# Scaling k, q and v weights inside their high/low split, column by column of the norm weight

## Chip, cores and metric

One core of one Trainium2 chip. The time is that of one execution on the device, in microseconds. All data is float32.

## The reference

A two-layer decoder trunk on 1024 tokens of width 1024. Layer 0 is gated linear attention and a gated MLP with a causal convolution of width 3. Then one shared K and V is projected from the stream, and layer 1 is differential attention on it (8 heads, two softmax maps each) and a second MLP. Each projection reads a normed stream, and the norms here have a weight per channel:

```
def rmsnorm(x, w):
    y = x * rsqrt(mean(x * x, axis=-1) + EPS)
    return y * w
kv = rmsnorm(h, kv_norm_w) @ w_kv            # -> k (rotary), v
q  = rope(rmsnorm(h, attn_norm_w[1]) @ w_q)
```

The channel weight w multiplies rows of w_kv and w_q, so it can be taken into them. The kernel does so for k, q and v, because k and v have one norm weight and q another while all three read the same stream.

## The kernel before

Activations are kept transposed, channels on the 128 partitions. A float32 product is made of three products of rounded parts (`fp32r`): each operand is split into a high part, made by a ScalarE copy into `fp32r`, and a low part, the rest, made by VectorE's `scalar_tensor_tensor` (helper `lo_of`, recorded at L114): low = x * scale - high. TensorE then accumulates high*high, low*high and high*low in PSUM (`proj_half`, L275 to L277; `v_block`, L1188 to L1190).

**Weights.** `plan` lists every weight tile in the order of use. `emit_load` issues its DMA into one of four `raw` buffers; `emit_split` makes (wh, wl) from it; `take` returns the oldest finished pair and calls `prefetch`, which splits and loads ahead (one ahead during the attention). A tile is 128x1024: for k and q it holds the eight channel blocks (k = 0 to 7) of 128 output columns, for v two channel blocks of 512 columns. The plan's entry (gi, k0, nk) names the norm weight, the first block and the number of blocks: (G_KV, 2j, 2) for eight tiles of v, (G_KV, 0, 8) and (G_ATTN1, 0, 8) for eight tiles each of k and q. `gains_sb[:, gi, d]` is a column of 128 norm weights. For these 24 tiles VectorE first multiplies the raw tile in place by the broadcast columns (L194, recorded at L111 as `raw<-raw,gains_sb`), then ScalarE copies the whole tile to wh (L195) and VectorE writes wl.

**Order.** ScalarE, TensorE and the DMA queue (SP) run in the order in which the program is written (`manual_schedule`). VectorE and GpSimd are put in order by a planner, which works with its own estimates of durations and with the program's order as priority, so that a VectorE instruction can be placed well ahead of its neighbours in the source.

**The attention stage.** After v (v_unit, 16 blocks) and k and q of heads 0 and 1, a loop over 64 steps (8 heads of 8 query blocks) does, in each step: the scores of block i two steps ahead into two PSUM buffers (`scores`, tile `sp`), the transposes of the weights (`turn`, tiles `tp`, `ah`, `al`), the combining of the two maps (`combine`, VectorE, tile `e`), and `weights`: VectorE's maximum of each map (`mx`) and ScalarE's exponential (`e`), after which the PSUM buffers are free for later scores. Into the steps are spread the projections of k and q of heads 2 to 7 in half units (`rope_unit`, tile `pf`), 8 units a head. The first unit of a projection calls `take`, which makes the split of the next tile. GpSimd does the rest of the rotary (`xw<-xw,sinr`, `y<-y,xw`, 128x1024) and the low parts of each head's q, k and v (`xl`).

Of the kernel before, what the change touches and what calls it, by code (L numbers as in the profile page):

```python
# [12 lines left out]
AF = mybir.ActivationFunctionType  # L13
ALU = mybir.AluOpType
AX = mybir.AxisListType

P = 128
# [30 lines left out]
def trunk(  # L48
# [26 lines left out]
    PE, ACT, DVE, POOL = nc.tensor, nc.scalar, nc.vector, nc.gpsimd  # L75
# [14 lines left out]
    def U(name, dt=F32):  # L90
        return up.tile([P, 1026], dt, tag="u", name=uid(name))[:, 0:1024]
# [18 lines left out]
    def tt(eng, o, a, b, op):  # L110
        eng.tensor_tensor(out=o, in0=a, in1=b, op=op)  # L111

    def stt(eng, o, a, s, b, op0, op1):
        eng.scalar_tensor_tensor(out=o, in0=a, scalar=s, in1=b, op0=op0, op1=op1)  # L114

    def lo_of(eng, lo, x, hi, scale=1.0):
        stt(eng, lo, x, scale, hi.bitcast(F32), ALU.mult, ALU.subtract)
# [5 lines left out]
    gains_sb = const.tile([P, 6, ND], F32, name="gains_sb")  # L123
# [6 lines left out]
    def gain(g, d):  # L130
        return gains_sb[:, g, d:d + 1]
# [30 lines left out]
    loaded, ready = deque(), deque()  # L162
# [3 lines left out]
    def emit_load():  # L166
        *srcs, g = plan[nxt[0]]
        nxt[0] += 1
        raws = []
        for src in srcs:  # L170
            raws.append(rawtile("raw"))
            nc.sync.dma_start(raws[-1], src)
        loaded.append((raws, g))

    def emit_split(eng=None):
        eng = eng or WENG
        if pair:
            emit_piece()
            return
        if not loaded:  # L180
            emit_load()
        raws, g = loaded.popleft()
        if g == "pair":
            pair.append(pieces(*raws) if len(raws) == 2 else pieces_by_form(raws[0:2], raws[2:4]))
            emit_piece()
            return
        raw, = raws
        hi = U("wh", F32R)
        lo = U("wl", F32R)
        if g is not None:  # L190
            gi, k0, nk = g
            rv = raw.rearrange("p (k n) -> p k n", k=nk)
            gb = gains_sb[:, gi, k0:k0 + nk].unsqueeze(2).broadcast_to([P, nk, 1024 // nk])
            tt(eng, rv, rv, gb, ALU.mult)  # L194
        ACT.activation(hi, raw, AF.Copy)  # L195
        if eng is POOL:
            tt(POOL, lo, raw, hi.bitcast(F32), ALU.subtract)
        else:
            lo_of(DVE, lo, raw, hi)
        ready.append((hi, lo))  # L200
# [21 lines left out]
    def pieces(ra, rg):  # L222


        a11, a12, s3, a22, s1, s2 = sums(ra, rg)
        yield halves(a11, "wp")
        yield halves(s2, "wp")
        tt(POOL, s2, a12, s2, ALU.subtract)
        yield halves(a12, "wp")
        yield halves(s3, "wp")  # L230
        yield halves(s1, "wp")
        yield halves(a22, "wp")
        pair.clear()
        yield halves(s2, "wp")

    def pieces_by_form(*raws):

        held[0] = True
        xs = [sums(*r) for r in raws]
        for q in (0, 1):  # L240
            for x in xs:
                yield halves(x[q], "wp")
        for a11, a12, s3, a22, s1, s2 in xs:
            tt(POOL, a12, a12, s2, ALU.subtract)
        for q in (1, 4, 5, 2, 3):
            held[0] = q == 1
            for x in xs:
                if q == 3 and x is xs[-1]:
                    pair.clear()
                yield halves(x[q], "wp")  # L250

    def emit_piece():
        ready.append(next(pair[0]))

    def prefetch(n, eng=None):
        while len(ready) < n and (pair or loaded or nxt[0] < len(plan)):
            emit_split(eng)
        while nxt[0] < len(plan) and (not loaded and not held[0] if plan[nxt[0]][-1] == "pair" else
                                      len(loaded) + len(ready) < max(n, LOADS)):
            emit_load()  # L260
# [237 lines left out]
    for d in range(ND):  # L498
        t = U("x")
# [309 lines left out]
    for hf in range(2):  # L809
        for d in range(ND):  # L810
# [7 lines left out]
            t = hx[d]  # L818
# [664 lines left out]
    for s in range(-2, steps + 5):  # L1483
        a, i = divmod(s + 2, NB)
# [5 lines left out]
        b, j = divmod(s - 1, NB)  # L1490
        if 0 <= s - 1 < steps and j % 2 == 1:
            heads[b].values(j // 2)
        b, j = divmod(s, NB)
        if 0 <= s < steps:
            heads[b].turn(j)
        if 0 <= s + 1 < steps:
            b, j = divmod(s + 1, NB)
# [19 lines left out]
        if 0 <= s - 2 < steps:  # L1517
            b, j = divmod(s - 2, NB)
# [4 lines left out]
        if 0 <= s - 3 < steps:  # L1523
            b, j = divmod(s - 3, NB)
            if j == NB - 1:
                heads[b].norm2()
        if 0 <= s - 4 < steps:
            b, j = divmod(s - 4, NB)
# [126 lines left out]
```

## Time and profile before

| | us |
|---|---|
| median of 3 runs | 2475.18 (2474.6 to 2475.31) |
| the profiled execution | 2473.61 |
| its span, first to last instruction | 2471.9 |
| TensorE busy | 2341.2 (95%) |
| VectorE busy | 1899.2 (77%) |
| ScalarE busy | 1039.0 (42%) |
| GpSimd busy | 837.4 (34%) |

PE is TensorE (PEld its weight loads), DVE VectorE, ACT ScalarE, POOL GpSimd. A row of a timeline gives the start and the length of an instruction, its engine, line and operation, out<-in, shapes, count, and in brackets the idle time of the engine before it with what ended it. Lengths include time in which a started instruction is held up. The attention stage lies between about 1240 and 1760 us.

### The profile page before, as it was taken

The page shows a single profiled execution, that of the slowest core. Times are in us where ns is not written, and L with a number is a line of the kernel's source. Part 1 is how long each engine was busy: PE and PEld are TensorE (multiplying, and loading weights), DVE is VectorE, ACT ScalarE, POOL GpSimd, SP SyncE. Part 2 cuts the span into 40 slices and gives each one's busy share as a digit, 9 for nine tenths or more (in the row PEclk, how much of TensorE's full clock was granted, in tenths as well). Part 3 has the DMA queues.
Part 4 walks back from the last instruction along what each step waited for, and adds up shares of the span by engine and source line. Part 5 has one row for each costly group of instructions (what it writes and reads, how often), then busy time and mean ns, then how long its engine had stood idle before and what let it go on. Part 6 is the DMA issues. An engine that isn't in the chain of part 4 may idle for free. (4 is left out here: it accounts for less than half of the span.)

```text
span 2471.9 us, 29625 instructions
## 1 busy us (share of the span) xinstructions
PE 2341.2 (95%) x10926; PEld 1888.5 (76%) x10926; DVE 1899.2 (77%) x2509; ACT 1039.0 (42%) x1856; POOL 837.4 (34%) x659
## 2 busy tenths in 40 slices
PE   8999999799999998999999999899789999998998
PEld 6878877577888886788877777787667888886786
DVE  7454454779999998957148888776779999999966
ACT  5433442433444344444124555544334433343453
POOL 3210101145554428400004444522036545436501
PEclk9999999899999999999999999999989999999999
DMA  4011224122333356324243333522113323256422
GB/s 178 1 52 69 70 93 149 42 68 95 111 110 99 111 200 230 117 71 165 81 138 106 107 111 95 182 75 94 67 34 120 119 82 111 92 192 222 144 88 98
DMA packets 101426, 271.22 MB, mean 110 GB/s; under 512 B 10273, under 2 KB 23201, under 8 KB 101281
## 3 DMA queue, kind: packets, MB, share of 16 engines
q1 hardware_dynamic: 101280, 269.34, 32.3%
q8 instruction: 85, 1.39, 0.2%
q14 instruction: 61, 0.49, 0.1%
HBM read 184.89 MB, written 76.02 MB: 106 GB/s over the span
## 5 line engine op out<-in xcount | busy, mean ns | idle before, releaser
L896 PE MATMUL pf<-xp,wp 128*128 128x512 f32 x1232 | 489.2, 397 | 37.4 <-ACT wp L205 33.2
L897 PE MATMUL pf<-xp,wp 128*128 128x512 f32 x1232 | 489.0, 397 | 7.1 <-DVE wp L114 7.1
L898 PE MATMUL pf<-xp,wp 128*128 128x512 f32 x1232 | 488.6, 397 | 0.0
L896 PEld LDWEIGHTS pf<-xp,wp 128*128 128x128 f32 x1232 | 233.1, 189 | 94.0 <-ACT wp L205 34.3
L897 PEld LDWEIGHTS pf<-xp,wp 128*128 128x128 f32 x1232 | 233.1, 189 | 64.3 <-DVE wp L114 9.1
L898 PEld LDWEIGHTS pf<-xp,wp 128*128 128x128 f32 x1232 | 233.0, 189 | 54.8
L1007 PE MATMUL out<-rp,lp 128*128 128x512 f32 (+1 forms) x632 | 251.1, 397 | 19.1 <-DVE rp L114 18.8
L1006 PE MATMUL out<-rp,lp 128*128 128x512 f32 (+1 forms) x632 | 250.1, 396 | 6.3 <-DVE lp L114 6.3
L114 DVE SCALAR_TENSOR_TENSOR c<-u,cv,c 128x1024 f32<-128x1024 f32 x176 | 244.7, 1392 | 7.6 <-ACT c L903 7.6
L1005 PE MATMUL out<-rp,lp 128*128 128x512 f32 (+1 forms) x632 | 249.9, 395 | 0.6 <-ACT rp L205 0.6
L111 DVE TENSOR_TENSOR u<-pf,u 128x512 f32<-128x512 f32 x300 | 200.4, 679 | 28.3 <-PE pf L898 20.1
L114 DVE SCALAR_TENSOR_TENSOR wp<-raw,wp 128x512 fp32r<-128x512 f32 x180 | 203.0, 1139 | 12.9 <-ACT wp L205 12.9
L275 PE MATMUL pf<-xh,wh 128*128 128x512 f32 x458 | 187.5, 409 | 10.7 <-ACT wh L195 9.7
L276 PE MATMUL pf<-xh,wl 128*128 128x512 f32 x458 | 181.9, 397 | 1.2 <-DVE wl L114 1.2
L277 PE MATMUL pf<-xl,wh 128*128 128x512 f32 x458 | 181.4, 396 | 0.0
L1007 PEld LDWEIGHTS out<-rp,lp 128*128 128x128 f32 x632 | 121.3, 192 | 51.6 <-DVE rp L114 24.6
L111 POOL TENSOR_TENSOR rs_y<-rs_m,nhalf 128x4 f32<-128x4 f32 (+2 forms) x26 | 31.9, 1226 | 370.9 <-DVE rs_m L291 301.7
L923 ACT ACTIVATE c<-c 128x1024 f32<-128x1024 f32 x44 | 46.7, 1061 | 255.7 <-DVE c L114 255.7
L114 DVE SCALAR_TENSOR_TENSOR wp<-wt,wp 128x512 fp32r<-128x512 f32 x128 | 153.6, 1204 | 0.0
L1006 PEld LDWEIGHTS out<-rp,lp 128*128 128x128 f32 x632 | 120.8, 191 | 36.8 <-DVE lp L114 9.8
L111 POOL TENSOR_TENSOR wt<-raw,wt 128x512 f32<-128x512 f32 x40 | 57.0, 1425 | 254.5 <-DVE wp L114 254.5
L1005 PEld LDWEIGHTS out<-rp,lp 128*128 128x128 f32 x632 | 121.3, 192 | 27.6 <-ACT rp L205 1.1
(252 smaller groups left out, 5170.5 us busy)
## 6 DMA issues: line engine op xcount, KB each, us to landing
raw<-in_w_in SPq DMA_DIRECT2D x88, 512.0 KB, 4.2
tr<-td SPq DMA_DIRECT2D x70, 512.0 KB, 4.1
td<-c SPq DMA_DIRECT2D x44, 512.0 KB, 2.8
wo<-in_w_out SPq DMA_DIRECT2D x44, 512.0 KB, 8.5
raw<-in_w_gla SPq DMA_DIRECT2D x24, 512.0 KB, 5.9
h<-hs SPq DMA_DIRECT2D x24, 512.0 KB, 6.5
td<-mt SPq DMA_DIRECT2D x22, 512.0 KB, 3.8
hs<-h SPq DMA_DIRECT2D x32, 256.0 KB, 2.0
```

The source lines that it names most:

```text
L111: eng.tensor_tensor(out=o, in0=a, in1=b, op=op)
L114: eng.scalar_tensor_tensor(out=o, in0=a, scalar=s, in1=b, op0=op0, op1=op1)
L275: PE.matmul(o, wh[:, k], xh[:, H(hf)], start=(k == 0), stop=False)
L276: PE.matmul(o, wl[:, k], xh[:, H(hf)], start=False, stop=False)
L277: PE.matmul(o, wh[:, k], xl[:, H(hf)], start=False, stop=(k == ND - 1))
L896: PE.matmul(o, wh, xh, start=(k == 0), stop=False)
L897: PE.matmul(o, wl, xh, start=False, stop=False)
L898: PE.matmul(o, wh, xl, start=False, stop=(k == ND // 2 - 1))
L923: ACT.activation(gt, gt, AF.Silu)
L1005: PE.matmul(o, wh, xh, start=(j == 0 or cut and j == NJ - LASTF), stop=False)
L1006: PE.matmul(o, wl, xh, start=False, stop=False)
L1007: PE.matmul(o, wh, xl, start=False, stop=(j == NJ - 1 or cut and j == NJ - LASTF - 1))
```

## The change

For a tile with a norm weight, the multiplication of the whole tile is gone. ScalarE makes the high part block by block, with the column of the norm weight as its scale, and VectorE the low part block by block, with the same column as its scalar: two blocks of 128x512 for v, eight of 128x128 for k and q, first all of ScalarE's, then all of VectorE's. The raw tile is no longer written. Other tiles are split as before.

```diff
         if g is not None:
             gi, k0, nk = g
-            rv = raw.rearrange("p (k n) -> p k n", k=nk)
-            gb = gains_sb[:, gi, k0:k0 + nk].unsqueeze(2).broadcast_to([P, nk, 1024 // nk])
-            tt(eng, rv, rv, gb, ALU.mult)
+            parts = [tuple(t.rearrange("p (k n) -> p k n", k=nk)[:, k] for t in (hi, lo, raw)) for k in range(nk)]
+            for k, (a, _, x) in enumerate(parts):
+                ACT.activation(a, x, AF.Copy, scale=gain(gi, k0 + k))
+            for k, (a, b, x) in enumerate(parts):
+                lo_of(DVE, b, x, a, gain(gi, k0 + k))
+            ready.append((hi, lo))
+            return
         ACT.activation(hi, raw, AF.Copy)
```

## Rows read from the trace of the kernel before

**Rows 1.** The page's part 1: busy us (share of the span) xinstructions of each engine.
```profile
PE 2341.2 (95%) x10926; PEld 1888.5 (76%) x10926; DVE 1899.2 (77%) x2509; ACT 1039.0 (42%) x1856; POOL 837.4 (34%) x659
```
**Rows 2.** Stretches: length, busy us of PE, PEld, DVE, ACT, POOL; clock, DMA share, GB/s.
```profile
1150.00:1240.00 90.00, 90.00 (x397) 73.00 (x396) 20.43 (x30) 18.79 (x25) 1.01 (x1) 1.00 0.28 96
...
1330.00:1460.00 130.00, 125.44 (x801) 101.83 (x798) 108.25 (x172) 68.60 (x159) 55.48 (x42) 1.00 0.32 98
```
**Rows 3.** The same view in steps of 10 us, about 1300.
```profile
1300.00:1310.00 10.00, 5.89 (x28) 4.53 (x27) 8.65 (x10) 1.94 (x5) 3.30 (x2) 0.81 0.42 133
1310.00:1320.00 10.00, 10.00 (x53) 8.09 (x52) 7.56 (x10) 6.17 (x12) 5.72 (x4) 0.85 0.43 131
```
**Rows 4.** Groups by line, 1130 to 1900: busy us, mean ns | idle before, releaser.
```profile
L111 DVE TENSOR_TENSOR raw<-raw,gains_sb 128x1024 f32<-128x1024 f32 x24 | 42.1, 1762 | 11.4 <-DMA raw<-in_w_v 7.7 <-DMA raw<-in_w_k 3.7
...
L195 ACT ACTIVATE wh<-raw 128x1024 fp32r<-128x1024 f32 x32 | 34.0, 1069 | 34.7 <-DVE raw L111 34.6
```
**Rows 5.** Timeline of ACT: four scaled copies of 128x256 in the first stage.
```profile
110.02 1.71 ACT L698 ACTIVATE wg<-wg,ro 128x256 f32<-128x256 f32 x4 [2.49 <-DVE ro L111]
```
**Rows 6.** Timeline of DVE: operations of 128x128 and their neighbour.
```profile
1294.32 0.35 DVE L114 SCALAR_TENSOR_TENSOR e<-e,rc 128x128 f32<-128x128 f32 x1
...
1297.75 0.28 DVE L114 SCALAR_TENSOR_TENSOR al<-tp,ah 128x128 fp32r<-128x128 f32 x1
1297.94 0.21 DVE L114 SCALAR_TENSOR_TENSOR rc<-s,nlam,rc 128x1 f32<-128x1 f32 x1
```
**Rows 7.** Timeline of DVE in the first FFN.
```profile
604.74 1.18 DVE L114 SCALAR_TENSOR_TENSOR wp<-raw,wp 128x512 fp32r<-128x512 f32 x1
605.85 1.78 DVE L114 SCALAR_TENSOR_TENSOR wp<-wt,wp 128x512 fp32r<-128x512 f32 x1
```
**Rows 8.** Timeline of POOL there.
```profile
605.34 1.74 POOL L111 TENSOR_TENSOR raw<-raw,raw 128x512 f32<-128x512 f32 x1
```
**Rows 9.** Timeline of DVE in one head of the attention.
```profile
1342.32 1.21 DVE L114 SCALAR_TENSOR_TENSOR wl<-raw,wh 128x1024 fp32r<-128x1024 f32 x1
...
1365.14 2.78 DVE L114 SCALAR_TENSOR_TENSOR wl<-raw,wh 128x1024 fp32r<-128x1024 f32 x1 [0.56 <-ACT wh L195]
1367.84 0.94 DVE L1329 TENSOR_REDUCE mx<-sp 128x1 f32<-128x768 f32 x1
...
1370.23 3.42 DVE L111 TENSOR_TENSOR raw<-raw,gains_sb 128x1024 f32<-128x1024 f32 x1
```
**Rows 10.** Timeline of POOL in that head.
```profile
1364.24 2.60 POOL L111 TENSOR_TENSOR xl<-st,xh 128x1024 fp32r<-128x1024 f32 x1 [4.12 <-ACT xh L314]
...
1367.08 3.04 POOL L111 TENSOR_TENSOR xw<-xw,sinr 128x1024 f32<-128x1024 f32 x1
1370.21 2.37 POOL L111 TENSOR_TENSOR y<-y,xw 128x1024 f32<-128x1024 f32 x1
```
**Rows 11.** Timeline of PE in that head: rows with idle time.
```profile
1371.32 0.50 PE L1312 MATMUL sp<-xh,xh 64*128 64x512 f32 x1 [0.31 <-ACT e L1330]
...
1375.62 0.51 PE L275 MATMUL pf<-xh,wh 128*128 128x512 f32 x1 [0.33 <-DVE osb L114]
...
1379.18 0.50 PE L1312 MATMUL sp<-xh,xh 64*128 64x512 f32 x1 [0.50 <-ACT e L1330]
1380.19 0.49 PE L1312 MATMUL sp<-xh,xh 64*128 64x512 f32 x1 [0.51 <-ACT e L1330]
```
**Rows 12.** Timeline of PE in the last head with a split: rows with idle time.
```profile
1576.76 0.49 PE L1312 MATMUL sp<-xh,xh 64*128 64x512 f32 x1 [0.30 <-ACT e L1330]
...
1590.34 0.38 PE L1312 MATMUL sp<-xh,xh 64*128 64x256 f32 x2 [1.50 <-ACT e L1330]
```
**Rows 13.** Timeline of DVE in the first attention steps.
```profile
1300.98 2.81 DVE L114 SCALAR_TENSOR_TENSOR e<-e,rc 128x384 f32<-128x384 f32 x1
```
**Rows 14.** Timeline of POOL there.
```profile
1298.28 2.65 POOL L111 TENSOR_TENSOR xw<-xw,sinr 128x1024 f32<-128x1024 f32 x1 [13.32 <-DVE rc L114]
```
**Rows 15.** Timeline of PE there.
```profile
1306.52 0.79 PE L1312 MATMUL sp<-xh,xh 64*128 64x512 f32 x1 [4.11 <-ACT e L1330]
```

## The prediction

> **What bounds the kernel now.** I read the page's busy times first: TensorE is busy 95% of the span and VectorE 77% [rows 1], so a change to VectorE and ScalarE work can pay or cost only where TensorE waits for them. The table of stretches says where that is. All of v's projection (1150 to 1240) runs with TensorE busy 90.00 of 90 us while VectorE has 20.4 and ScalarE 18.8 us of work; from 1330 to 1460, where k's and q's projections are spread over the attention steps, TensorE idles 4.56 us and VectorE is busy 108 of 130 [rows 2]. The table in 10 us steps shows one worse spot: in 1300 to 1310 TensorE is busy 5.89 us and its granted clock falls to 0.81, then 0.85 [rows 3], below the upper of its two levels. So the 24 changed tiles fall in two sorts: eight of v, whose cost is hidden, and sixteen of k and q, most of them beside the attention.
>
> **Part by part.**
>
> *Removed:* 24 VectorE multiplications of 128x1024, mean 1.76 us [rows 4], although a VectorE split of the same size, with two SBUF sources too, takes 1.21 when nothing holds it [rows 9]. That is 42 us of VectorE. What makes them long is GpSimd: the multiplication at 1370.23 lasts 3.42 us, and GpSimd's y runs from 1370.21 for 2.37 [rows 9, 10]. VectorE instructions with two SBUF sources and GpSimd's tensor ops wait for each other whole.
>
> *ScalarE:* one copy of 1.07 us [rows 4] becomes, for k and q, eight of 128x128 with a column as scale. Four such of 128x256 span 1.71 us, 0.495 the single one [rows 5], so (1.71 - 0.495) / 3 = 0.405 from start to start; 128 columns fewer are about 0.1 ((1.07 - 0.495) / 768 per column), so 0.3 each and 2.4 a tile: 1.4 more. ScalarE next waits for the maxima of the scores, which are later still (below), so I take nothing for it; without that cover it would be 1.4 a tile.
>
> *VectorE's split:* one of 1.2 us alone becomes eight of 128x128. A split of that size starts 0.19 before the next instruction; an operation of that size with a column scalar and two SBUF sources lasts 0.35 whole [rows 6]. Between them I take 0.25 (0.19 to 0.35), so 2.0 a tile (1.5 to 2.8). [...]
>
> *v's eight tiles:* two instructions for one on each engine, one multiplication less. TensorE has no idle time there [rows 2], and VectorE and ScalarE are three quarters idle: nothing, either way.
>
> *The sixteen of k and q, the wait that counts.* Next to each split is a queue of GpSimd work (xl, then the rotary xw and y). In each of five heads (k's tile, split starting at 1315, 1365, 1417, 1468 and 1519, all of 2.77 or 2.78 us) the order is that of rows 9: the split, held by xl until 1366.71 (1365.14 + 2.78 - 1.21), then the maximum of the next scores at 1367.84, for which the exponentials and with them TensorE's score products wait: TensorE stands 0.31 at 1371.32 [rows 11]. There is no slack, so what the split adds goes to TensorE. xw asks at 1367.08 and gets its turn after 0.67 us (3.04 - 2.37), when the split is done [rows 10]. With eight pieces it need not wait: only one or two are done by 1367.08. Which goes first at such an instant is shown in the FFN: GpSimd asks at 605.34 while VectorE's split runs until 605.92; VectorE's next split, started at 605.85 without a pause, lasts 1.78 instead of 0.68, while GpSimd's operation lasts 1.74 [rows 7, 8]. The one that waits gets the next gap, even in a row of VectorE instructions. So xw goes between the pieces: 2.37 us, and then six pieces, 1.5: the maximum starts at about 1367.25 + 2.37 + 1.5 = 1371.1, 3.3 late. Below: if nothing cuts in, 1366.71 + 2.0, 0.9 late, or zero and less if the planner, which orders VectorE anew, puts the maximum ahead. Above: y cuts in too, another 2.37, 5.6 late. I take one cut, 3.3. [...]
>
> *What comes back:* with the multiplication at 1370.23 gone, 3.4 us of VectorE are free just behind the late maximum, so the next maxima are on time again and the stalls of 0.33, 0.50 and 0.51 [rows 11] go: 1.34. One head shows that already: its tile belongs to the output projection and has no multiplication, and after 0.30 at 1576.76 TensorE's next wait is at 1590.34 [rows 12]. The three rows recur in three of the five heads: 4.0 us.
>
> *q's tiles* lie where TensorE has room (1330 to 1460 holds two k tiles, whose stalls of rows 11 sum to 2 x 1.65 of the 4.56 idle in rows 2, and 0.6 a head is left for all else): nothing, at most one GpSimd operation of 2.37 each.
>
> *The first attention steps:* at 1300.98 a combine of 384 columns lasts 2.81 us beside GpSimd; the exponentials come late and TensorE waits 4.11 at 1306.52 [rows 13 to 15]. It starts right behind GpSimd's xw (1298.28 + 2.65 = 1300.93) and is then held by the next one. Ahead of it VectorE has a multiplication and a split, 2.4 us; after, 2.0 of pieces, while GpSimd is idle until 1298.28. So it comes 0.4 earlier or more, against a GpSimd start that waits for a transfer and doesn't move; the rows don't say whether that is enough to be ahead of it. If it is, 4.11 go and the lower clock with them (5.89 x 0.19 + 10 x 0.15 = 2.6): -6.7. If not, 0. I take half, -3.4.
>
> *Clock:* a stall of 3.6 in each head may bring the clock down as the 4.11 did: 0 to 5 x 2.6 = 13. I take 0, as the nearest row has the longer stall.
>
> *Sum:* 5 x 3.3 - 4.0 - 3.4 = +9.1. The profiled execution took 2473.6 (span 2471.9 and 1.7 around it): 2482.7. The median of the runs is 1.6 above it: 2484.
>
> **Rivals.**
> *A, the row of pieces isn't cut* (the planner puts the maxima ahead of them, or VectorE keeps its turn): the late maximum costs 0 to 0.9, the multiplications' 1.3 a head come back, the start stall goes: -4.0 - 6.7 = -10.7, 2464.5; with 0.9 a head, 2469. For it: 42 us less on the engine that ends TensorE's waits, and the head of rows 12. Against it: the FFN's rows 7 and 8.
> *B, all nearly cancels:* the cut costs 0.9 to 2 a head and is paid by the stalls that go: 5 x 1.5 - 4.0 - 3.4 = 0, 2475. For it: TensorE's waits there are 2.2 a head in all. Against it: no row has the maximum with slack.
> *C, the forecast's mechanism in full:* two cuts in each head and the clock with them, 5 x 5.6 - 4.0 + 13 = +37, 2512. It decides where y's request comes within one piece of xw's end; before, it came 0.09 after it (1367.08 + 3.04 to 1370.21).
>
> **How the numbers follow.** Forecast with its upper side C 0.50 (C alone 0.12), A 0.28, B 0.22. Up to 0.2%, 5 us, can't be told from no change. A is faster, B the same, the forecast and C slower: 0.28, 0.22, 0.50. The likeliest one's own range is 2478 (the start stall gone whole, 0.5 a head less) to 2497 (a clock fall in each head). The range for 8 in 10 reaches down to A's 2465 and up to 2503, most of the way to C.
>
> **What would show it.** Right: eight pieces of wl in a row between 1365 and 1372 with one piece of 2.5 us or more and xw beside it, the 768-column maximum 2 to 4 us later in the head, stalls of 2 to 4 us at the 896-column scores and none at the next. Wrong: pieces of 0.3 us throughout, xw waiting for several of them, or the maximum between them; TensorE's idle time in the attention under that of before. If v's stretch shows TensorE idle, or ScalarE is what the maxima's readers wait for, my terms of nothing fail.

## The result, and the profile after

The changed kernel takes 2506.03 us (median of 4 runs, 2505.21 to 2508.99); the kernel before, run beside it on the same chip, takes 2474.89 (2473.95 to 2475.31). The ratio is 1.0128, with an interval of 1.0115 to 1.0141: slower by 31 us. The profiled execution after took 2505.44 (span 2503.7), the one of before 2473.6 (span 2471.9), so the two profiles carry the difference: 31.8 in the span.

Part 1 of the page after: busy us, share of the span, instructions of each engine.

```profile
PE 2352.2 (94%) x10926; PEld 1902.5 (76%) x10926; DVE 1905.4 (76%) x2605; ACT 1060.5 (42%) x1976; POOL 825.5 (33%) x659
```

Read against [rows 1], this line splits the loss. TensorE does the same 10,926 matmuls and is busy 11.0 us longer (2352.2 - 2341.2). Its idle time is 2503.7 - 2352.2 = 151.5, where it was 2471.9 - 2341.2 = 130.7: 20.8 more. 11.0 + 20.8 = 31.8, the whole difference. VectorE lost 24 multiplications and is busy 6.2 us longer; GpSimd, whose work did not change, is busy 11.9 us less, because it waits less: xw and y of the rotary take 2.46 and 2.38 us in the mean where they took 2.74 and 2.82.

The stretch from the first score product to the end of the last `pv` product (1285.3 to 1702.3 before, 1285.8 to 1734.2 after) holds 2477 matmuls in both traces. First before, then after (length, busy us of PE, PEld, DVE, ACT, POOL; clock, DMA share, GB/s):

```profile
1285.30:1702.30 417.00, 392.04 (x2477) 318.60 (x2478) 332.80 (x545) 214.28 (x483) 161.02 (x119) 0.98 0.35 112
1285.80:1734.20 448.40, 400.03 (x2477) 329.75 (x2478) 349.25 (x611) 227.53 (x560) 151.60 (x119) 0.94 0.33 104
```

So 31.4 of the 31.8 us lie in the attention. There TensorE is busy 8.0 us longer for the same matmuls, at a mean granted clock of 0.94 instead of 0.98, and idle 23.4 longer (448.40 - 400.03 against 417.00 - 392.04). Of the 11.0 us above, 3.0 lie ahead of v's projection, where no changed tile is used, with 2.4 us less idle time: the two executions differ there. Any split into busy and idle time is only as good as the matmuls' modelled ends; the sum is exact.

The groups by line, 1130 to 1800, that stand where those of [rows 4] stood (busy us, mean ns | idle before, releaser):

```profile
L114 DVE SCALAR_TENSOR_TENSOR wl<-raw,gains_sb,wh 128x128 fp32r<-128x128 f32 x128 | 84.7, 722 | 5.7 <-ACT wh L194 5.7
L194 ACT ACTIVATE wh<-raw,gains_sb 128x128 fp32r<-128x128 f32 x128 | 39.1, 402 | 5.5 <-DMA raw<-in_w_k 5.5
```

A piece of 128 columns takes 722 ns in the mean, more than half of what a whole split of 1024 takes when nothing holds it (1.21 us, [rows 9]).

The stretches (length, busy us of PE, PEld, DVE, ACT, POOL; clock, DMA share, GB/s):

```profile
1150.00:1240.00 90.00, 90.00 (x398) 73.29 (x397) 14.66 (x40) 22.48 (x43) 1.01 (x1) 1.00 0.27 93
1330.00:1460.00 130.00, 115.68 (x731) 95.36 (x730) 103.83 (x181) 70.31 (x180) 47.58 (x39) 0.95 0.30 90
```

v's projection is as it was [rows 2]. From 1330 to 1460 TensorE gets through 731 matmuls where it did 801, with 14.3 us idle instead of 4.6 and a clock of 0.95 instead of 1.00. The same view in steps of 10 us, beside [rows 3]:

```profile
1300.00:1310.00 10.00, 8.48 (x48) 6.72 (x49) 7.58 (x13) 4.82 (x14) 1.17 (x1) 1.00 0.54 162
1310.00:1320.00 10.00, 6.39 (x38) 4.65 (x36) 9.81 (x13) 4.82 (x13) 7.57 (x5) 0.87 0.35 120
1320.00:1330.00 10.00, 7.50 (x37) 6.59 (x38) 6.35 (x11) 3.44 (x8) 0.00 (x0) 0.61 0.31 88
1370.00:1380.00 10.00, 4.75 (x27) 4.12 (x27) 10.00 (x13) 2.51 (x7) 6.09 (x5) 0.78 0.13 52
1380.00:1390.00 10.00, 10.00 (x64) 8.06 (x64) 7.51 (x14) 5.45 (x12) 0.90 (x1) 0.88 0.37 107
1430.00:1440.00 10.00, 4.77 (x24) 3.77 (x22) 9.30 (x16) 2.47 (x5) 2.81 (x2) 0.68 0.13 52
```

Each line with VectorE at 9.3 to 10.0 is a tile of k. TensorE works half to two thirds of such a stretch, and its granted clock is 0.87, 0.78 and 0.68 there, and 0.61, 0.88 and 0.98 (1440 to 1450) in the line behind it; between 1370 and 1390, in steps of 1 us, it is 0.50 from 1376 to 1382, and 1.00 up to 1375 and from 1383 on. Before, it was 1.00 in all of these stretches but the first two, those of [rows 3], where in steps of 1 us it was 0.50 from 1307 to 1313.

What happens in one head is in the timelines. VectorE, where [rows 9] stood (start us, us, engine, line, operation, out<-in, count, and in brackets the idle time ahead):

```profile
1292.82 1.66 DVE L114 SCALAR_TENSOR_TENSOR wl<-raw,gains_sb,wh 128x128 fp32r<-128x128 f32 x6
...
1296.01 0.34 DVE L114 SCALAR_TENSOR_TENSOR wl<-raw,gains_sb,wh 128x128 fp32r<-128x128 f32 x1
...
1367.97 0.88 DVE L114 SCALAR_TENSOR_TENSOR e<-e,rc,e 128x640 f32<-128x640 f32 x1
1368.78 7.80 DVE L114 SCALAR_TENSOR_TENSOR wl<-raw,gains_sb,wh 128x128 fp32r<-128x128 f32 x5
1376.50 0.94 DVE L1333 TENSOR_REDUCE mx<-sp 128x1 f32<-128x768 f32 x1
1377.37 0.86 DVE L114 SCALAR_TENSOR_TENSOR wl<-raw,gains_sb,wh 128x128 fp32r<-128x128 f32 x3
1378.15 0.68 DVE L114 SCALAR_TENSOR_TENSOR al<-tp,ah 128x512 fp32r<-128x512 f32 x1
...
1399.36 5.47 DVE L114 SCALAR_TENSOR_TENSOR wl<-raw,gains_sb,wh 128x128 fp32r<-128x128 f32 x4
```

The first row is a stretch beside which GpSimd does nothing: six pieces in 1.66 us; the second is a single piece, 0.34. Five pieces in the head take 7.80. GpSimd fills the difference (this fence answers to [rows 10]):

```profile
1368.51 2.60 POOL L111 TENSOR_TENSOR xl<-st,xh 128x1024 fp32r<-128x1024 f32 x1 [4.11 <-ACT xh L318]
...
1371.36 2.39 POOL L111 TENSOR_TENSOR xw<-xw,sinr 128x1024 f32<-128x1024 f32 x1
1373.83 2.34 POOL L111 TENSOR_TENSOR y<-y,xw 128x1024 f32<-128x1024 f32 x1
...
1399.67 2.52 POOL L111 TENSOR_TENSOR xw<-xw,sinr 128x1024 f32<-128x1024 f32 x1 [3.33 <-DMA xw<-xsb]
1402.28 2.40 POOL L111 TENSOR_TENSOR y<-y,xw 128x1024 f32<-128x1024 f32 x1
```

xl is under way when the first piece starts, and xw and y go in between the pieces that follow; the row ends only when y does (1373.83 + 2.34 = 1376.17); the maximum starts at 1376.50. GpSimd's xw lasts 2.39 where it lasted 3.04: it has stopped waiting, and VectorE waits instead. The last two rows stand beside the four pieces of q's tile at 1399.36. TensorE, beside [rows 11] and [rows 15]:

```profile
1301.51 0.44 PE L1362 MATMUL tp<-ident,e 128*128 128x128 f32 x2 [2.41 <-DVE e L114]
...
1318.43 0.79 PE L1316 MATMUL sp<-xh,xh 64*128 64x512 f32 x1 [2.83 <-ACT e L1334]
1322.49 0.79 PE L1316 MATMUL sp<-xh,xh 64*128 64x512 f32 x1 [3.27 <-ACT e L1334]
...
1350.70 0.39 PE L1376 MATMUL pv<-ah,xh 128*128 128x256 f32 x1 [1.34 <-DVE al L114]
...
1378.88 2.08 PE L312 MATMUL rb<-ident,ro 128*128 128x128 f32 x8 [5.25 <-DVE al L114]
```

`rb` is the norm's broadcast; it waits for `al`, the low half of the transposed probabilities, which stands on VectorE behind the late maximum and three more pieces (1378.15 + 0.68 = 1378.83). TensorE's waits (us in total, times, longest), 1240 to 1660 after:

```profile
PE rb L312 <- DVE al L114: 21.0, 4, 5.3
PE sp L1316 <- ACT e L1334: 10.7, 14, 3.3
PE pv L1376 <- DVE al L114: 6.7, 5, 1.4
```

The same before, 1240 to 1640 (the line numbers shift with the edits):

```profile
PE sp L1312 <- ACT e L1330: 14.7, 26, 4.1
PE pf L275 <- DVE osb L114: 1.0, 3, 0.3
PE pv L1372 <- DVE al L114: 0.6, 1, 0.6
```

Before, no wait of `rb` was there at all.

### The profile page after: what moved, and what is told of

Read it like the earlier page. It is cut to its first block, busy times and chain, and to the rows that moved or that the text cites. A ratio compares the mean times of both kernels' runs of the same rounds, so it can differ in the third digit from the quotient of the medians.

```text
span 2503.7 us, 29852 instructions
## 1 busy us (share of the span) xinstructions
PE 2352.2 (94%) x10926; PEld 1902.5 (76%) x10926; DVE 1905.4 (76%) x2605; ACT 1060.5 (42%) x1976; POOL 825.5 (33%) x659
```

## Experiments

The theory tested first: a VectorE instruction with two SBUF sources is a place at which a waiting GpSimd instruction of about 2.4 us can go first, so eight of them for one tile let in what one kept out. Its rivals: the 120 extra ScalarE copies (1976 - 1856), a fixed cost of small VectorE instructions, or the place of the split in the queue. All times stand against the kernel before, run beside them.

**Pieces alone, in eight and in two.** The multiplication and the whole copy on ScalarE stay; only the low half is cut up (e1_lo8 with 8, shown here; e2_lo2 with `n = 1024 // 2`), for v, k and q.

```diff
+            ACT.activation(hi, raw, AF.Copy)
+            n = 1024 // 8
+            for k in range(0, 1024, n):
+                lo_of(DVE, lo[:, k:k + n], raw[:, k:k + n], hi[:, k:k + n])
+            ready.append((hi, lo))
+            return
```

> The kernel before, with its multiplication and its whole high part, but the low part in eight VectorE instructions of 128 columns (v's tiles too). Theory 1 (each GpSimd tensor operation that waits goes into the next gap between VectorE's pieces, so a row of eight lets three in where one let in one): slower than before by 25 to 45 us, since the multiplications stay as well; TensorE's stalls at k's tile about 5 us. Theory 2 (ScalarE's eight scaled copies, 2.4 us a tile in place of 1.1, are what comes late): within 4 us of before, since ScalarE's part is whole here. Theory 3 (nothing but the fixed cost of small VectorE instructions, 0.8 us a tile): 4 us slower at most.

> The kernel before with the low part in two VectorE instructions of 512 columns, the multiplication kept. Theory 1: one gap in each split, so one more GpSimd operation of 2.4 us ahead of the maximum in each of five heads: 8 to 15 us slower than before, well under half of the eight-piece kernel's loss. Theory 2: as before. Theory 3: 0.1 us a tile, as before.

Eight: 2498.65 (2498.07 to 2504.55) against 2477.31, ratio 1.0091 (1.0076 to 1.0106), +21. Two: 2489.52 (2488.96 to 2491.55), ratio 1.0051 (1.0034 to 1.0068), +12. Eight came under the 25 to 45 that were expected, two inside the 8 to 15, though at more than half the loss of eight. A row of VectorE in a head with eight, and TensorE's wait behind it:

```profile
1368.10 7.61 DVE L114 SCALAR_TENSOR_TENSOR wl<-raw,wh 128x128 fp32r<-128x128 f32 x8 [0.56 <-ACT wh L195]
```

```profile
PE rb L314 <- DVE al L114: 19.6, 4, 4.9
```

The same two lines with two pieces:

```profile
1368.52 5.02 DVE L114 SCALAR_TENSOR_TENSOR wl<-raw,wh 128x512 fp32r<-128x512 f32 x2 [0.56 <-ACT wh L195]
```

```profile
PE rb L314 <- DVE al L114: 9.3, 4, 2.3
```

The same 1024 columns last 2.78 whole [rows 9], 5.02 in two, 7.61 in eight: each step is one GpSimd instruction (2.24 and 2.59): xl alone beside the whole split, xl and xw beside two pieces, xl, xw and y beside eight. The wait of the broadcast goes 0, 2.3, 4.9. With the same multiplication and the same copy, the number of pieces alone makes the wait of the changed kernel. In the stretch of 2477 matmuls (1282.4 to 1726.7) this kernel of eight takes 444.3 us with 396.2 busy, so TensorE is idle 48.1, as long as in the changed one (48.4). Of the 4.1 us between the two stretches 3.8 are busy time. The losses of 21 and 31 us differ by more than that; how much of the rest is the change and how much one execution against another is not shown.

**ScalarE's copies alone.** The multiplication and the whole low half stay; the high half is made by eight copies with a column of ones as scale.

```diff
+            for k in range(0, 1024, P):
+                ACT.activation(hi[:, k:k + P], raw[:, k:k + P], AF.Copy, scale=ones[:, 0:1])
+            lo_of(DVE, lo, raw, hi)
+            ready.append((hi, lo))
+            return
```

> The kernel before with the high part in eight ScalarE copies of 128 columns, with a column of ones as scale, and the low part whole, after the multiplication. Theory 1: within 4 us of before, as VectorE's split stays one instruction (it starts up to 1.4 us later, while GpSimd holds it anyway). Theory 2: 7 to 20 us slower, as much of the changed kernel's loss as ScalarE makes.

2468.91 (2467.1 to 2470.76), ratio 0.9964 (0.9951 to 0.9977): 8.4 us faster. ScalarE's small copies are not the loss, and no wait of the broadcast is in this trace. That they gain was not expected (within 4 us was). The multiplications are shorter there, and the order on VectorE is another. The group of the multiplications, and the stretch of 2477 matmuls:

```profile
L111 DVE TENSOR_TENSOR raw<-raw,gains_sb 128x1024 f32<-128x1024 f32 x24 | 31.7, 1323 | 11.2 <-DMA raw<-in_w_v 7.4 <-DMA raw<-in_w_k 3.3 <-DMA raw<-in_w_q 0.4
```

```profile
1286.00:1696.20 410.20, 387.31 (x2477) 317.53 (x2478) 326.00 (x545) 227.80 (x560) 162.35 (x119) 0.99 0.36 113
```

1323 ns against 1762 [rows 4] fits instructions that meet GpSimd less often. The stretch is 6.8 us shorter than before: 4.7 of it busy time (392.04 - 387.31), which fits the higher clock, and 2.1 idle time. From 1300 to 1320 the granted clock is 1.00 there, where it was 0.81 and 0.85 [rows 3]. Why the small copies lead to this was not settled.

**The scaling on ScalarE, the split whole.** ScalarE multiplies the tile in place by columns; then one copy and one VectorE split.

```diff
-            gb = gains_sb[:, gi, k0:k0 + nk].unsqueeze(2).broadcast_to([P, nk, 1024 // nk])
-            tt(eng, rv, rv, gb, ALU.mult)
+            for k in range(nk):
+                ACT.activation(rv[:, k], rv[:, k], AF.Copy, scale=gain(gi, k0 + k))
```

> The multiplication goes to ScalarE, block by block and in place, then the high part and the low part whole as before: ScalarE has 3.4 us a tile in place of 1.1, VectorE one instruction of 1.2. Theory 1: 4 to 11 us faster than before, as VectorE loses 42 us and its split has no gap. Theory 2: slower than the changed kernel's loss by ScalarE's further 1 us a tile, 30 to 45 us over before.

2465.96 (2464.21 to 2469.81), ratio 0.9955 (0.9941 to 0.997): 11.4 us faster than before, just above the 4 to 11 that were expected, some 40 faster than the change, and the best of all that ran. ScalarE's part of a head:

```profile
1357.58 2.44 ACT L194 ACTIVATE raw<-raw,gains_sb 128x128 f32<-128x128 f32 x8
1360.05 1.06 ACT L195 ACTIVATE wh<-raw 128x1024 fp32r<-128x1024 f32 x1
```

VectorE's:

```profile
1358.31 1.82 DVE L1329 TENSOR_REDUCE mx<-sp 128x1 f32<-128x768 f32 x2 [0.19 <-PE sp L1314]
1361.14 2.64 DVE L114 SCALAR_TENSOR_TENSOR wl<-raw,wh 128x1024 fp32r<-128x1024 f32 x1 [1.01 <-ACT wh L195]
```

ScalarE carries 1.06 more a tile than in the change; the split waits for its copy, and both maxima stand ahead of it. The split takes one wait for GpSimd, not two or three, and the broadcast waits 1.6 at most (6.2 in four heads). So taking the multiplication from VectorE does pay, once the split is one instruction.

**The changed kernel with its splits elsewhere.** In three kernels the split of k's tiles is issued one half unit of the projections later, and that of q's two: the changed kernel (e5_after_late), the ScalarE one (e6_act_late) and the one before (e7_before_late).

```diff
-    rp, tails, stores = {}, deque(), deque()
+    rp, tails, stores, late = {}, deque(), deque(), [0]
...
         if hf == 0 and part == 0:
-            rp["w"] = take()
+            rp["w"] = ready.popleft()
+            late[0] = 2 if dst in kd else 1
+        elif late[0]:
+            late[0] -= 1
+            if late[0] == 0:
+                prefetch(AHEAD)
+        if hf == 0 and part == 0:
```

> The changed kernel, with the same eight pieces, but each split moved to a later half unit of its projection: k's one unit later (behind the 768-column exponentials), q's two (behind the 384-column ones), where the trace shows GpSimd idle or nearly done. Theory 1 (pieces cost what GpSimd's operations between them cost): the loss of 31 us goes down to 8 or less, or turns into a gain (2468 to 2483), with pieces of about 0.3 us. Rival (small instructions are dear by themselves, or ScalarE's eight copies are): 2495 to 2508, as the counts are the same.

> The multiplication on ScalarE in place, the split whole, and the splits moved as in the late kernel. Theory 1: the 1.55 us stalls at k's tile and the 0.2 at q's go, 5 to 10 us under the kernel with the multiplication on ScalarE alone (2456 to 2461). Rival (the place in the step is right as it is): the same as that kernel or slower, 2466 to 2475.

> The kernel before, with its multiplication, and the splits moved in the same way. Theory 1: the whole split was held by one GpSimd operation of 1.6 us at k's tile; 3 to 10 us faster than before if it now stands free (2466 to 2473). Rival: the moved loads and splits cost as much elsewhere, 2473 to 2482.

Against 2476.39: the changed one 2478.68 (2476.94 to 2481.19), ratio 1.0013 (1.0003 to 1.0022); the ScalarE one 2475.33 (2471.6 to 2479.63), ratio 0.9996 (0.9985 to 1.0007); the one before 2483.83 (2481.76 to 2487.25), ratio 1.0036 (1.0023 to 1.0048). The move by itself costs the kernel before 7.4 us, where a gain of 3 to 10 was expected. The loss of the change goes from 31 to 2.3, and in the moved place the change is 5.2 us faster than what it replaces (2478.68 - 2483.83). VectorE and the group of pieces in the changed one:

```profile
1372.43 2.93 DVE L114 SCALAR_TENSOR_TENSOR wl<-raw,gains_sb,wh 128x128 fp32r<-128x128 f32 x3
```

```profile
L114 DVE SCALAR_TENSOR_TENSOR wl<-raw,gains_sb,wh 128x128 fp32r<-128x128 f32 x128 | 51.4, 459 | 10.4 <-ACT wh L194 10.1
```

A piece is 459 ns in the mean instead of 722 (about 300 were expected), and in the attention's heads a tile of k is cut only by y. The ScalarE kernel, which was expected to gain 5 to 10 by the move, lost 9.4 (2475.33 - 2465.96, not run beside each other). The move brings new waits of the projection for the rotary results, 5.6 us in four heads, where there was no such wait; what the rest of the 9.4 is was not followed.

**The multiplication on GpSimd.**

```diff
-            tt(eng, rv, rv, gb, ALU.mult)
+            tt(POOL, rv, rv, gb, ALU.mult)
```

> The multiplication goes to GpSimd (one operation of some 2.4 us a tile), high and low part whole. Theory 1: VectorE loses 42 us of its own work, but 24 more GpSimd operations hold its instructions with two SBUF sources whole: between 8 us faster and 10 us slower than before. Rival (VectorE's amount of work is what counts): 8 to 12 us faster, as with the multiplication on ScalarE.

2469.82 (2466.66 to 2472.8), ratio 0.9975 (0.9966 to 0.9984): 6.6 faster, with 24 more GpSimd instructions of 2.30 us. This lies inside theory 1's range and a little under the rival's. As with the ScalarE kernel, VectorE without the multiplication and with a whole split is a gain.

**The cutting instructions taken away.** The rotary xw and y go to VectorE, in the changed kernel (e9_after_ropedve) and in the one before (e10_before_ropedve).

```diff
-        eng = eng or SIDE
+        eng = eng or DVE
```

> The changed kernel, its splits in their places, but the rotary's xw and y of the attention stage on VectorE in place of GpSimd: two of the three GpSimd operations beside k's tile are gone, and VectorE has 24 more of 1.2 us. Theory 1: only xl is left to hold the pieces, so it lies within 8 us of the kernel before with the same edit (on either side), where without the edit 31 us lie between the two. Rival (small instructions, or ScalarE's copies, are dear by themselves): still 20 us or more over that kernel. The time itself may be anywhere from 2470 to 2500, as VectorE has 29 us more to do.

> The kernel before with the rotary's xw and y of the attention stage on VectorE: the control for the changed kernel with this edit. All theories: VectorE has 29 us more and fewer instructions held by GpSimd, 2470 to 2500.

2489.8 (2484.71 to 2494.45), ratio 1.0053 (1.0033 to 1.0073), and 2485.42 (2481.33 to 2487.96), ratio 1.0032 (1.002 to 1.0045), against 2476.46. Both of these kernels are slower than the kernel before as it stands, and are compared with each other: with xw and y off GpSimd the change costs 4.4 us (2489.8 - 2485.42), not 31. The pieces in the head of the first, and their group:

```profile
1359.47 3.53 DVE L114 SCALAR_TENSOR_TENSOR wl<-raw,gains_sb,wh 128x128 fp32r<-128x128 f32 x5
```

```profile
L114 DVE SCALAR_TENSOR_TENSOR wl<-raw,gains_sb,wh 128x128 fp32r<-128x128 f32 x128 | 47.3, 427 | 5.9 <-ACT wh L194 5.9
```

Five pieces take 3.53 with xl alone beside them, 7.80 with xl, xw and y: 4.27 for two instructions. This is the plainest evidence for the cuts. Part of the wait is left: with xl beside the pieces the broadcast waits 14.2 us for `al` in the first of the two, and 6.1 in its control. The kernel before spreads from 2471 to 2481 beside the moved splits and from 2473 to 2481 here, so the 4.4, and the 2.3 above, are near what can be told.

## Why the prediction was wrong

The direction held, and so did the mechanism that GpSimd's instructions go in between the pieces. How many go in, what comes late by them, q's tiles and the clock were taken too small, and the 9.1 became 31.

*The multiplication removed, v's tiles, ScalarE's copies:* as forecast. The 24 instructions are gone, v's stretch is 90.00 of 90, and eight copies span 2.44 (2.4 was the estimate), with no TensorE wait in the attention traced to them:

```profile
1368.33 2.44 ACT L194 ACTIVATE wh<-raw,gains_sb 128x128 fp32r<-128x128 f32 x8
```

*Cost of a piece:* right at 0.26 where nothing cuts in ((1.66 - 0.34) / 5, the last piece whole at 0.34; 0.25 was taken).

*The cut into k's pieces, the step that failed:* one cut and 3.3 us a head were taken, two cuts and 5.6 were the upper bound. Both xw and y went in. The maximum started 8.53 after the combine did (1376.50 - 1367.97); before, it was 4.14 (1367.84 [rows 9] against the row below) with the one wait for xl that was there already: 4.4 late. It is less than 5.6 mainly because the planner put the maximum after five pieces, not eight. The other three then stood ahead of `al`, and in four heads `al`, not the maximum, held the first TensorE reader: 5.25 a head. In the first head it was the exponentials, behind the maximum as forecast: 2.83 + 3.27. That is 27.1 in all instead of 16.5. The condition that the prediction gave for two cuts, y's request within one piece of xw's end, was met: y starts 0.08 after xw's end (1371.36 + 2.39 to 1373.83), and before the change it was 0.09 [rows 10]. The row that decided it was on the table and got too small a chance. The combine before:

```profile
1363.70 0.88 DVE L114 SCALAR_TENSOR_TENSOR e<-e,rc,e 128x640 f32<-128x640 f32 x1
```

*What comes back:* the later stalls of the head (0.33, 0.50 and 0.51, [rows 11]) are gone. TensorE's waits for the exponentials, without the first attention step's 4.11 and the first tile of k's 6.1, fell from 10.6 (14.7 - 4.1) to 4.6, and the 1.0 for `osb` went too: 7.0 less in all, where the forecast was 4.0 less.

*q's tiles:* nothing was taken, with one GpSimd instruction of 2.37 each as the most. In three of the five heads two went in: four of the eight pieces at 1399.36 lasted 5.47, beside xw and y. In the other two y alone did, behind an xw that had held the instruction ahead of the pieces. `al` stands behind the row, and `pv` waits for it in all five heads, 1.34 each: 6.7 us where 0.6 were. With xw and y on VectorE (e9_after_ropedve) none of these waits is left.

*The first attention steps:* half of 4.11 and its clock was taken. The 4.11 gave way to 2.41 and the clock in 1300 to 1310 stayed at 1.00 [rows 3], so the term itself was about right; the first k tile's 6.1 us, twenty microseconds on, took it back with a clock of 0.61.

*The waits together:* 27.1 for k's tiles and 6.1 for q's, less 7.0 that came back and 1.7 at the first steps, are 24.5; the stretch of the attention has 23.4 more idle time.

*Clock:* nothing was taken, 0 to 13 were the bounds. It cost about 8.0 (TensorE's busy time in the attention, for 2477 matmuls in both). The nearest row had a stall of 4.11 [rows 15] and a lower clock behind it; with 5.25 in each head that row applied, and setting the term to zero rested wholly on the 3.3 that was too small. So one misjudged cut was paid twice: in the stall and in the clock.

*The rivals:* A needed the row not to be cut; it was, in every head. That an uncut removal gains was right (the whole split with ScalarE's scaling gained 11.4 where A gave 10.7). C, two cuts in each head and the clock with them, was given as 2512 and is the one that happened, at 2506. That its time came so near is in part luck: it had the clock too high (13 for 8.0) and nothing for q's tiles (6.1).

Open: why the small ScalarE copies alone gain 8.4 us, why the loss of eight pieces alone is 10 us smaller than that of the change, and how far idle time and clock can be told apart in the 31.8.

## What to carry to other kernels

Count, ahead of a change, how many VectorE instructions with two SBUF sources will stand next to a queue of GpSimd tensor operations: here one that waited could go in whole at a start (xw, 2.39, and y, 2.34, between the pieces at 1368.78), so splitting one of 1.2 us into eight added two more waits of 2.4 at k's tiles, where the saved multiplication was 1.76. If a per-column scale is wanted there, give the pieces to an engine outside that contest (here ScalarE, 2.44 us for eight beside xl at 1368.33, 2.45 at 1288.98 with GpSimd idle) and leave the contested engine one instruction. And where a stall of several microseconds is forecast in every head, price the clock with it when a row of the same trace shows it.

## What the runs showed of the hardware

- A GpSimd instruction that asks while VectorE works through a row of two-source instructions went in at the next start, and the next waiting one after it, with 0.26 us pieces between: 7.80 us for five pieces with three such instructions, 3.53 with one, 1.66 for six with none. GpSimd does not go first every time: before the change the whole split that starts at 1342.32 lasts its free 1.21 [rows 9], and y, which starts 0.01 us behind it, waits for it:

```profile
1342.32 3.47 POOL L111 TENSOR_TENSOR y<-y,xw 128x1024 f32<-128x1024 f32 x1
```

- What GpSimd held were VectorE instructions with two SBUF sources. From 1240 to 1760 before, 14 of the 15 whole splits and multiplications of k's, q's and the output's tiles that started inside xl, xw or y lasted 2.77 to 3.43 us and ended 1.08 or 1.09 after it; the 15th, at 1473.38, lasted 1.21, and y waited. The 16 that met none of them lasted 1.21 to 1.23. `al` of 128x512, with a source in PSUM (`tp`), lasted 0.67 to 0.69 both inside one (22 times) and clear of them (25).
- VectorE's pieces of 128x128 overlap: 0.34 us long each, 0.26 from start to start in the uncut row.
- At the four stalls of 5.25 us the lowest granted clock of a 10 us stretch was 0.78, 0.68, 0.66 and 0.68; after two of 2.83 and 3.27 close together it was 0.61. A single wait of 3.15 us at 1302.56, in the kernel with the small ScalarE copies, left it at 1.00.
- The clock's cost can be read from two stretches with equal counts of matmuls: 8.0 us more busy time at a mean clock of 0.94 instead of 0.98. Ahead of v's projection, where the two kernels do the same, the two executions differ by 3.0.
